# Decoder layer in float32: the last products' sums kept apart, accumulators loaded later

## The chip, the cores and the metric

One core of a Trainium2 chip runs the whole program. The metric is the device time of one execution in microseconds (us). Engines are named PE or TensorE (matmuls), DVE or VectorE, ACT or ScalarE, POOL or GpSimd, and SP, which issues most DMAs.

## The reference

One decoder layer on x of 1024 tokens by 1024 channels, in float32:

```
x <- LN1(alpha*x + 0.5*SwiGLU_1(x))
x <- LN2(alpha*x + W_out [ SparseAttn(x) || ChunkedGMLP(x) ])
x <- LN3(alpha*x + 0.5*SwiGLU_2(x))
SwiGLU(x) = (silu(x @ w1) * (x @ w3)) @ w2        # w1, w3: 1024 x 2816, w2: 2816 x 1024
```

Both SwiGLU layers run through the same function of the kernel; the change is in that function alone. The mixer in the middle (top-k attention and gMLP) is not touched.

## The kernel before

**Precision.** A float32 operand is split into two parts of type fp32r: hi (a ScalarE copy, L87) and lo (the difference, L88, on VectorE or GpSimd). `mm3` (L112 to L114) multiplies with three matmuls: hi by hi, hi by lo, lo by hi.

**Seven products.** `ffn` computes each large product by a 2x2 scheme with seven products of blocks in place of eight (Strassen's, in the form of Winograd). Products are numbered 1 to 7, and the factors and results are sums and differences of blocks.

**First products** (x @ w1, x @ w3). The 2816 hidden channels are 11 groups of two 128-wide blocks. `product(g, m)` is one of the seven products of group g: 24 matmuls into a pair of PSUM banks (tile `ab`; there are two pairs). Products 1 and 2 of groups 0 to 5 run ahead of everything else ("early"); their sums go to DRAM (`spill`), and so does the first part of the hidden block (`hid`). `group(g)` then runs the other products, for g from 1 on in the order 6, 7, 5, 4, 3, adds them on VectorE (u2 at L340, u3 at L375, c at L378), and stores the hidden block to `hid`. Within `group(g)` the next group is loaded: u2 and h1 of an early group (L347, L348) from `spill` and `hid`, and four weight blocks `w` (L300), numbered 1, 2, 7, 4. `left` makes the left factors some three products ahead; S (L248) is the first sum of a group's blocks and needs blocks 7 and 4. Outputs are L402 to L407.

**Second product** (hidden @ w2). Tokens are two halves of four 128-token tiles, the output has two column halves of 512, and k runs over the 11 groups. For each product m but the last, k is the outer loop and the four token tiles j the inner one: 12 matmuls per k. Results gather in four PSUM banks X (tile `y`) for products 1, 2, 5, 4 or four banks Y (tile `z`) for 6, 3, 7. Product 2 may go on top of 1, 7 on top of 3, and 4 on top of 5. For product 4, j is the outer loop (33 matmuls per tile). `prepare` makes the pieces (hi and lo of the hidden block `a` and of the weight block `b`) five ahead; `weights` makes sums of the weight blocks b11, b12, b21, b22 in place on VectorE (L487 to L495). Product 6 needs a sum in a page of its own, `t` (L488).

**Accumulators.** The result is 8 token tiles `xacc` of 1024 columns: C11 and C12 are the column halves of the first four, C21 and C22 of the others. `load_acc` loads alpha*x into them (L591, scaled by ScalarE at L592) in product 1. GpSimd then takes differences (L468, via `each`): C21 - C22 and C22 - C12. `add2` (L530, VectorE) adds half of a product's banks to one quarter: product 1, 6, 5 and 3 to C12, 2 to C11, 7 to C22, 4 to C21. After product 3 GpSimd adds C12 to C22, and after product 7 C22 to C21, which undoes the differences. So what three of the quarters share is added once. `norm` (layernorm) of tiles 0 to 3 runs in product 7, of tiles 4 to 7 after each tile of product 4.

**Order.** Instructions are written in program order and each engine's queue is then ordered by a planner, which simulates the engines with its own costs and takes the earliest in program order among what is ready. Pages (4 KB per partition, 21 of them: weight blocks, factors, pieces, `t`, `xacc`, u2, h1, layernorm rows) and PSUM banks are handed out in that order too. Every engine and the DMA queue of SP run their instructions in order.

Of the kernel before, what the change touches and what calls it, by code (L numbers as in the profile page):

```python
# [12 lines left out]
AF = mybir.ActivationFunctionType  # L13
# [21 lines left out]
class Net:  # L35
# [181 lines left out]
    def ffn(self, name, w13, w2, begin, meanwhile, load_acc, norm, after):  # L217
# [111 lines left out]
        def group(g, begun=None):  # L329
            then = due.append if g == 0 else lambda f: f()  # L330
            if begun:
                h1, h11 = begun
            else:
                a = pair()
                sums[g], h1 = first(g, a), page("h1")
                h11 = h1[:, 0]
            b = pair()
            product(g, 6, b)
            u2 = sums[g]
            then(lambda b=b: V.tensor_tensor(u2, b, sums[g], ALU.add))  # L340
            if not begun:
                product(g, 2, a, start=False)
                gated(h11, a)
            if g < NG - 1:
                if g + 1 < EARLY:
                    sums[g + 1], again[g + 1] = page("u2"), page("h1")
                    nc.sync.dma_start(sums[g + 1], spill[g + 1])  # L347
                    nc.sync.dma_start(again[g + 1][:, 0], hid[g + 1, :, 0])  # L348
                for m in (1, 2, 7, 4):
                    load(g + 1, m)  # L350
            u3, c, h2 = page("u3"), page("c22"), page("h2")
            if g == 0:
                a = pair()
                product(g, 5, a)
                then(lambda: V.tensor_tensor(c, a, u2, ALU.add))
                b = pair()
                product(g, 7, b)

                def out7(b=b):
                    V.tensor_tensor(c, b, c, ALU.add)  # L360
                    V.tensor_tensor(u3, b, u2, ALU.add)
                    gated(h2[:, 1], c)

                then(out7)
                product(g, 3, a, start=False)

                def out3():
                    V.tensor_tensor(u2, a, u2, ALU.add)
                    gated(h2[:, 0], u2)

                then(out3)
            else:
                b = pair()
                product(g, 7, b)
                V.tensor_tensor(u3, b, u2, ALU.add)  # L375
                a = pair()
                product(g, 5, a)
                V.tensor_tensor(c, a, u3, ALU.add)  # L378
                gated(h2[:, 1], c)
            b = pair()  # L380
            product(g, 4, b)
            h12, s4 = (u3[:, 0], u3[:, 1]) if g == 0 else (h1[:, 1], u3[:, 0])

            def out4():
                V.tensor_tensor(u3, b, u3, ALU.add)
                gated(h12, u3)

            then(out4)
            if g:
                product(g, 3, a, start=False)  # L390
                V.tensor_tensor(u2, a, u2, ALU.add)
                gated(h2[:, 0], u2)

            def out():
                e = E(PAR["HE"])
                s = c
                e.tensor_tensor(s[:, 0], h2[:, 0], h2[:, 1], ALU.add)
                e.tensor_tensor(s[:, 1], s[:, 0], h11, ALU.subtract)
                e.tensor_tensor(h2[:, 0], h11, h2[:, 0], ALU.subtract)
                e.tensor_tensor(s4, s[:, 1], h12, ALU.subtract)  # L400
                if g < EARLY:
                    nc.sync.dma_start(hid[g, :, 1], h12)  # L402
                else:
                    nc.sync.dma_start(hid[g, :, 0:2], h1)
                for i, t in enumerate((h2, s), 1):
                    nc.sync.dma_start(hid[g, :, 2 * i : 2 * i + 2], t)
                nc.sync.dma_start(hid[g, :, 6], s4)  # L407

            then(out)
# [53 lines left out]
        for k in range(NG):  # L463
            load2(k)

        def each(e, a, b, op):
            for x, y in zip(a, b):
                e.tensor_tensor(x, x, y, op)  # L468

        order2 = (1, 6, 2, 5, 3, 7, 4)  # L470
        plan2 = [(m, k) for m in order2[:5] for k in range(NG)]
        for k in range(NG + PAR["D4"]):
            if k < NG:
# [1 line left out]
            if k >= PAR["D4"]:  # L475
                plan2.append((4, k - PAR["D4"]))
        HID = {1: 0, 2: 1, 7: 2, 4: 3, 5: 4, 6: 5, 3: 6}
        raws, pieces, last = {}, {}, {}

        def weights(m, k):  # L480

            w = W[k]
            b11, b12, b21, b22 = w[:, 0, 0], w[:, 0, 1], w[:, 1, 0], w[:, 1, 1]
            e = E(PAR["W2S"])
            if m == 6:
                src = self.page("t2", (P, HALF))
                e.tensor_tensor(b11, b12, b11, ALU.subtract)  # L487
                e.tensor_tensor(src, b22, b11, ALU.subtract)  # L488
                return src
            if m == 2:  # L490
                e.tensor_tensor(b12, b22, b12, ALU.subtract)
            if m == 5:
                e.tensor_tensor(b21, b21, b11, ALU.add)
            if m == 3:
                e.tensor_tensor(b21, b22, b21, ALU.subtract)  # L495
            return {1: b11, 2: b21, 5: b11, 3: b22, 7: b12, 40: b21}[m]

        def prepare(n):
# [33 lines left out]
        for m in order2[:6]:  # L532
            if m in (1, 5):
                X = [self.bank("y") for _ in range(4)]
            if m in (6, 3):
                Y = [b[:, s] for b in (self.banks("z") for _ in range(2)) for s in (slice(0, HALF), slice(HALF, D))]
            ps = X if m in (1, 2, 5) else Y
            for k in range(NG):
                prepare(plan2.index((m, k)) + 1 + PAR["LP"])
                for j in range(4):  # L540
                    tile2(m, k, j, ps)
                if m == 1 and k == PAR["AQ"]:
                    acc = load_acc()
                    C11, C12 = ([acc[j][:, s] for j in range(4)] for s in (slice(0, HALF), slice(HALF, D)))
                    C21, C22 = ([acc[4 + j][:, s] for j in range(4)] for s in (slice(0, HALF), slice(HALF, D)))
                    each(E(PAR["CV"]), C21, C22, ALU.subtract)
                    each(E(PAR["CV"]), C22, C12, ALU.subtract)
                if m == 7 and k in PAR["NK"]:
                    t = PAR["NK"].index(k)
                    norm(t, acc[t])  # L550
            for j in range(4):
                add2({2: C11, 7: C22}.get(m, C12)[j], ps[j], -0.5 if m == 3 else 0.5)
            if m == 3:
                each(E(PAR["CV"]), C22, C12, ALU.add)
        each(E(PAR["CV"]), C21, C22, ALU.add)
        for j in range(4):
            for k in range(NG):
                prepare(plan2.index((4, k)) + 1 + PAR["LP"])
                tile2(4, k, j, X)
                if k == PAR["AK"]:  # L560
                    after(j, acc[j])
            add2(C21[j], X[j], -0.5)
            norm(4 + j, acc[4 + j])
        return [lambda t=t: after(t, acc[t]) for t in range(4, NT)]

# [18 lines left out]
                self.nc.tensor.transpose(ps[:, j * P : (j + 1) * P], src[:, k * P : (k + 1) * P], self.ident)  # L584
            self.nc.scalar.activation(self.x_block(((0, 1), (5, 2))[h][b])[:, :, cols], ps.rearrange("p (k c) -> p k c", k=4), AF.Copy)

    def load_acc(self, src):
        acc = []
        for t in range(NT):
            a = self.page("xacc")  # L590
            self.nc.sync.dma_start(a, src[t * P : (t + 1) * P, :])  # L591
            self.nc.scalar.activation(a, a, AF.Copy, scale=ALPHA)  # L592
            acc.append(a)
        return acc
# [542 lines left out]
    def run(self):  # L1137
        nc, ins = self.nc, self.ins
        x1 = self.dram.tile([T, D], F32, tag="x1", name="x1_spill")
        x2 = self.dram.tile([T, D], F32, tag="x2", name="x2_spill")  # L1140
        gb = {}

        def normed(n, dst):
            def norm(t, x):
                if n not in gb:
                    gb[n] = self.rows(f"ln{n}_g"), self.rows(f"ln{n}_b")
                last = n == 3 and t == NT - 1
                cut = PAR["CUT"][3] if last else PAR["CUT"][n - 1]
                self.layernorm(x, x, *gb[n], cut)
                for s in (slice(0, cut), slice(cut, D)) if last else (slice(0, D),):  # L1150
                    nc.sync.dma_start(dst[t * P : (t + 1) * P, s], x[:, s])

            return norm

        nothing = lambda n: None
        tail = self.ffn("f1", ins["ffn1_w13"], ins["ffn1_w2"], self.load_x, nothing, lambda: self.load_acc(ins["x"]), normed(1, x1), self.to_act)
        tail = self.mixer(x1, tail, normed(2, x2), self.to_x)

        def rest(n):
            tail[n]()  # L1160

        self.ffn("f2", ins["ffn2_w13"], ins["ffn2_w2"], nothing, rest, lambda: self.load_acc(x2), normed(3, self.out[0]), lambda t, x: None)


def layouts(i):
# [47 lines left out]
```

## Time and profile before

| | us |
|---|---|
| runs | 1799.16, 1801.49, 1802.94 (median 1801.49) |
| profiled execution | 1801.68 |
| its span | 1799.9 |
| TensorE busy | 1740.1 (97%) |
| VectorE busy | 1326.1 (74%) |
| ScalarE busy | 791.1 (44%) |
| GpSimd busy | 506.6 (28%) |

The span is the time from the first to the last instruction. Matmuls are pipelined, so a busy TensorE is told better by the matmuls in a stretch than by its busy time. The first layer's first products lie at 0 to 436 us, its second at 436 to 658; the last layer's at 1150 to 1573 and 1573 to 1790. The granted clock of TensorE in a stretch is 1.00 at full speed.

### The profile page before, as it was taken

To read this page: it belongs to the slowest core of one execution; us is meant where nothing else is said; L and a number is where in the kernel's file an instruction comes from. 1 tells how busy PE (TensorE), PEld (TensorE's weight loads), DVE (VectorE), ACT (ScalarE), POOL (GpSimd) and SP (SyncE) were. 2 spreads that over 40 slices of the span, in tenths; PEclk is the share of its full clock that TensorE was granted. 3 is DMA by queue.
4 is the path that set the end of the run, shared out by engine and by line. 5 is a ranking of instruction groups with operands and counts; after the bars stand their busy time and mean duration, and the time that the engine had idled before them with its cause. 6 is when DMAs were issued, how large, how long until landed. Compare 5 with 4: busy or idle time off the path is not lost.

```text
span 1799.9 us, 22286 instructions
## 1 busy us (share of the span) xinstructions
PE 1740.1 (97%) x8056; PEld 1459.8 (81%) x8056; DVE 1326.1 (74%) x2192; ACT 791.1 (44%) x1336; POOL 506.6 (28%) x368
## 2 busy tenths in 40 slices
PE   8999999999899999979998999999999999989997
PEld 6878888888788889978876888888788888878886
DVE  5776755666796865999979877877767555589786
ACT  5421322323454435678787763352222222355451
POOL 0013422221400462364247620100323222240035
PEclk9999999999999999989999999999999999999999
DMA  7445432238544332112620006435443322753532
GB/s 282 164 146 193 152 112 88 90 118 324 181 135 134 121 108 56 48 47 65 196 62 13 13 1 204 158 117 203 141 177 127 125 88 88 296 202 113 161 100 82
DMA packets 81790, 235.37 MB, mean 131 GB/s; under 512 B 8208, under 2 KB 8720, under 8 KB 81680
## 3 DMA queue, kind: packets, MB, share of 16 engines
q1 hardware_dynamic: 78320, 225.82, 35.9%
q0 software_dynamic: 1920, 2.89, 0.8%
q10 hardware_dynamic: 1440, 5.24, 0.8%
q8 instruction: 63, 1.03, 0.2%
q14 instruction: 47, 0.39, 0.1%
HBM read 168.64 MB, written 62.39 MB: 128 GB/s over the span
## 4 chain that ended last, share of the span: by engine, by line
PE 80%; DVE 9%; ACT 3%; DMA 3%; issue 3%; POOL 1%; SPq 0%; POOLq 0%; ACTq 0%; DVEq 0%
PE ab L112 14%; PE ab L114 14%; PE ab L113 14%; PE y L113 6%; PE y L112 6%; PE y L114 6%; PE z L113 3%; PE z L114 3%; PE z L112 3%; DMA w<-in_ffn_w_dram 2%; PE tr L986 1%; DVE dve L790 1%; ACT act L799 1%; PE ol L113 1%; PE ol L114 1%
## 5 line engine op out<-in xcount | busy, mean ns | idle before, releaser
L112 PE MATMUL ab<-xs,hi 128*128 128x512 f32 x1232 | 482.6, 392 | 13.4 <-DVE c L378 5.7
L113 PE MATMUL ab<-xs,hi 128*128 128x512 f32 x1232 | 481.8, 391 | 0.0
L114 PE MATMUL ab<-xs,lo 128*128 128x512 f32 x1232 | 481.5, 391 | 0.0
L88 POOL TENSOR_TENSOR lo<-w,hi 128x1024 fp32r<-128x1024 f32 x54 | 135.5, 2509 | 567.7 <-ACT hi L87 527.9
L112 PEld LDWEIGHTS ab<-xs,hi 128*128 128x128 f32 x1232 | 232.8, 189 | 63.3 <-issue 6.4
L113 PEld LDWEIGHTS ab<-xs,hi 128*128 128x128 f32 x1232 | 232.8, 189 | 48.9 <-DVE xs L88 0.4
L114 PEld LDWEIGHTS ab<-xs,lo 128*128 128x128 f32 x1232 | 232.7, 189 | 48.1
L87 ACT ACTIVATE hi<-w 128x1024 fp32r<-128x1024 f32 (+1 forms) x134 | 137.4, 1040 | 184.7 <-DVE w L251 137.1
L88 DVE TENSOR_TENSOR lo<-w,hi 128x1024 fp32r<-128x1024 f32 (+1 forms) x80 | 94.8, 1195 | 41.2 <-ACT hi L87 40.7
L307 ACT ACTIVATE h<-c 128x512 f32<-128x512 f32 x34 | 21.5, 631 | 202.3 <-DVE c L378 141.2
L113 PE MATMUL z<-b,a 128*128 128x512 f32 x264 | 105.2, 398 | 4.0 <-DVE b L88 4.0
L87 ACT ACTIVATE b<-w 128x512 fp32r<-128x512 f32 x110 | 68.9, 626 | 88.2 <-PE y L114 46.4
L112 PE MATMUL z<-b,a 128*128 128x512 f32 x264 | 102.5, 397 | 5.1 <-ACT b L87 5.1
L88 DVE TENSOR_TENSOR a<-hid,a 128x512 fp32r<-128x512 f32 x132 | 95.9, 726 | 12.9 <-ACT a L87 12.9
L114 PE MATMUL z<-b,a 128*128 128x512 f32 x264 | 104.4, 397 | 0.0
L114 PE MATMUL y<-b,a 128*128 128x512 f32 x264 | 102.8, 389 | 0.0
L113 PE MATMUL y<-b,a 128*128 128x512 f32 x264 | 102.8, 389 | 0.0
L799 ACT ACTIVATE act<-score,tk 128x768 int8<-128x768 f32 (+2 forms) x93 | 86.7, 932 | 33.7 <-DVE tk L811 28.8
L112 PE MATMUL y<-b,a 128*128 128x512 f32 x264 | 101.2, 390 | 0.0
L87 ACT ACTIVATE a<-hid 128x512 fp32r<-128x512 f32 x132 | 81.9, 620 | 40.3 <-DMA hid<-f 37.9
L88 DVE TENSOR_TENSOR b<-w,b 128x512 fp32r<-128x512 f32 x110 | 80.2, 730 | 24.1 <-ACT b L87 23.9
L468 POOL TENSOR_TENSOR xacc<-xacc,xacc 128x512 f32<-128x512 f32 x16 | 21.9, 1388 | 237.1 <-DVE xacc L530 236.8
(273 smaller groups left out, 3715.7 us busy)
## 6 DMA issues: line engine op xcount, KB each, us to landing
w<-in_ffn_w_dram SPq DMA_DIRECT2D x110, 512.0 KB, 6.1
hid<-f SPq DMA_DIRECT2D x60, 512.0 KB, 3.8
w<-in_ffn_w_dram SPq DMA_DIRECT2D x22, 1024.0 KB, 11.3
f<-h SPq DMA_DIRECT2D x32, 512.0 KB, 3.4
f<-c SPq DMA_DIRECT2D x22, 512.0 KB, 4.2
xr<-x_spill SPq DMA_DIRECT2D x16, 512.0 KB, 5.3
x_spill<-xr SPq DMA_DIRECT2D x16, 512.0 KB, 3.4
f<-u SPq DMA_DIRECT2D x24, 256.0 KB, 6.0
```

The source lines that it names most:

```text
L87: nc.scalar.activation(hi, src, AF.Copy)
L88: (eng or nc.vector).tensor_tensor(lo, src, hi.bitcast(F32), ALU.subtract)
L112: mm(out, a[0], b[0], start=start, stop=False, skip_group_check=skip)
L113: mm(out, a[0], b[1], start=False, stop=False, skip_group_check=skip)
L114: mm(out, a[1], b[0], start=False, stop=stop, skip_group_check=skip)
L307: nc.scalar.activation(t, c[:, 0], AF.Silu)
L468: e.tensor_tensor(x, x, y, op)
L790: V.tensor_scalar(self.marks("dve", s.shape[-1]), s, f, None, ALU.is_lt, ALU.add, accum_out=val[:, j : j + 1])
L799: nc.scalar.activation(out, s, AF.Sign, bias=fj, scale=-1.0, accum_out=val[:, j : j + 1])
L986: nc.tensor.transpose(pt[:, hh * P : (hh + 1) * P], ps4[hh][:, j * P : (j + 1) * P], self.ident)
```

## The change

1. Product 1's banks are copied by ScalarE, halved, to four half tiles T (two pages). Products 6, 5 and 3 are added to T. After product 3 GpSimd adds T to C12; after product 7 (also added to T) it adds T to C21 and C22. The differences of accumulators and their undoing are gone.
2. The order is 1, 2, 6, 5, 3, 7, 4. The weight sums of the blocks are made in products 2 and 6.
3. `load_acc` takes a range of tiles: four are loaded in product 2 and four in product 5, each at k = 2.
4. In the first products, u2 and h1 of the next early group are requested after this group's last product, no longer ahead of its weight blocks.

```diff
             if g < NG - 1:
-                if g + 1 < EARLY:
-                    sums[g + 1], again[g + 1] = page("u2"), page("h1")
-                    nc.sync.dma_start(sums[g + 1], spill[g + 1])
-                    nc.sync.dma_start(again[g + 1][:, 0], hid[g + 1, :, 0])
                 for m in (1, 2, 7, 4):
                     load(g + 1, m)
...
+            if g + 1 < EARLY:
+                sums[g + 1], again[g + 1] = page("u2"), page("h1")
+                nc.sync.dma_start(sums[g + 1], spill[g + 1])
+                nc.sync.dma_start(again[g + 1][:, 0], hid[g + 1, :, 0])
 
             def out():
...
-        def each(e, a, b, op):
-            for x, y in zip(a, b):
-                e.tensor_tensor(x, x, y, op)
-
-        order2 = (1, 6, 2, 5, 3, 7, 4)
+        order2 = (1, 2, 6, 5, 3, 7, 4)
...
+            if m == 2:
+                e.tensor_tensor(b11, b12, b11, ALU.subtract)
+                e.tensor_tensor(b12, b22, b12, ALU.subtract)
             if m == 6:
                 src = self.page("t2", (P, HALF))
-                e.tensor_tensor(b11, b12, b11, ALU.subtract)
                 e.tensor_tensor(src, b22, b11, ALU.subtract)
+                e.tensor_tensor(b21, src, b21, ALU.subtract)
                 return src
-            if m == 2:
-                e.tensor_tensor(b12, b22, b12, ALU.subtract)
-            if m == 5:
-                e.tensor_tensor(b21, b21, b11, ALU.add)
-            if m == 3:
-                e.tensor_tensor(b21, b22, b21, ALU.subtract)
...
-                if m == 1 and k == PAR["AQ"]:
-                    acc = load_acc()
-                    C11, C12 = ([acc[j][:, s] for j in range(4)] for s in (slice(0, HALF), slice(HALF, D)))
-                    C21, C22 = ([acc[4 + j][:, s] for j in range(4)] for s in (slice(0, HALF), slice(HALF, D)))
-                    each(E(PAR["CV"]), C21, C22, ALU.subtract)
-                    each(E(PAR["CV"]), C22, C12, ALU.subtract)
+                if (m, k) in ((2, 2), (5, 2)):
+                    acc += load_acc(range(len(acc), len(acc) + 4))
...
+            if m == 1:
+                T = [t[:, i] for t in (page("T"), page("T")) for i in range(2)]
             for j in range(4):
-                add2({2: C11, 7: C22}.get(m, C12)[j], ps[j], -0.5 if m == 3 else 0.5)
-            if m == 3:
-                each(E(PAR["CV"]), C22, C12, ALU.add)
-        each(E(PAR["CV"]), C21, C22, ALU.add)
+                if m == 1:
+                    nc.scalar.activation(T[j], ps[j], AF.Copy, scale=0.5)
+                elif m == 2:
+                    add2(acc[j][:, :HALF], ps[j])
+                else:
+                    add2(T[j], ps[j], -0.5 if m == 3 else 0.5)
+                if m == 3:
+                    nc.gpsimd.tensor_tensor(acc[j][:, HALF:], acc[j][:, HALF:], T[j], ALU.add)
+                if m == 7:
+                    for s in (slice(0, HALF), slice(HALF, D)):
+                        nc.gpsimd.tensor_tensor(acc[4 + j][:, s], acc[4 + j][:, s], T[j], ALU.add)
...
-            add2(C21[j], X[j], -0.5)
+            add2(acc[4 + j][:, :HALF], X[j], -0.5)
```

## Rows read from the trace of the kernel before

**Rows 1.** Slices: length, busy us (count) of PE, PEld, DVE, ACT, POOL; clock; DMA.
```profile
125.00:150.00 25.00, 21.41 (x84) 17.23 (x83) 15.72 (x16) 6.74 (x8) 10.02 (x4) 0.86 0.52 178
...
450.00:475.00 25.00, 22.45 (x99) 18.00 (x97) 18.82 (x29) 11.66 (x16) 19.12 (x8) 1.00 0.63 232
475.00:500.00 25.00, 23.00 (x91) 18.78 (x91) 21.96 (x37) 14.10 (x25) 0.00 (x0) 0.86 0.41 116
500.00:525.00 25.00, 25.00 (x112) 20.72 (x111) 25.00 (x43) 12.51 (x22) 0.00 (x0) 1.00 0.33 95
525.00:550.00 25.00, 25.00 (x112) 20.73 (x111) 21.17 (x35) 11.84 (x21) 0.00 (x0) 1.00 0.58 171
...
575.00:600.00 25.00, 25.00 (x112) 20.73 (x111) 20.63 (x31) 13.68 (x24) 5.49 (x4) 1.00 0.40 127
...
1250.00:1275.00 25.00, 22.93 (x102) 18.69 (x101) 18.78 (x18) 6.13 (x7) 4.81 (x2) 1.00 0.53 189
1600.00:1625.00 25.00, 20.44 (x79) 16.15 (x78) 18.04 (x28) 8.94 (x16) 11.65 (x8) 0.86 0.31 90
```

**Rows 2.** Waits of TensorE: line, what for, us in total, times, longest.
```profile
PE ab L112 <- DVE c L378: 5.7, 2, 3.6
...
PE z L112 <- ACT b L87: 5.1, 2, 2.6
PE z L113 <- DVE b L88: 4.0, 2, 2.0
```

**Rows 3.** TensorE in order of time, product 6: start, us, instruction.
```profile
477.66 0.63 PE L114 MATMUL z<-b,a 128*128 128x512 f32 x1
478.09 0.63 PE L112 MATMUL z<-b,a 128*128 128x512 f32 x1
```

**Rows 4.** VectorE in order of time, in brackets the idle time before.
```profile
466.79 0.69 DVE L530 SCALAR_TENSOR_TENSOR xacc<-y,xacc 128x512 f32<-128x512 f32 x1 [2.56 <-POOL xacc L468]
...
472.41 1.13 DVE L488 TENSOR_TENSOR t<-w 128x512 f32<-128x512 f32 x1
...
536.08 0.69 DVE L530 SCALAR_TENSOR_TENSOR xacc<-y,xacc 128x512 f32<-128x512 f32 x1
```

**Rows 5.** GpSimd in order of time: first and last of eight differences.
```profile
455.39 10.01 POOL L468 TENSOR_TENSOR xacc<-xacc 128x512 f32<-128x512 f32 x1 [36.67 <-ACT xacc L592]
...
473.07 1.60 POOL L468 TENSOR_TENSOR xacc<-xacc,xacc 128x512 f32<-128x512 f32 x1
```

**Rows 6.** Groups by line: count, then shortest, median and longest ns of one.
```profile
L468 POOL TENSOR_TENSOR xacc<-xacc x16: 1275/1296/10007, 455.4 to 1769.9; 128x512 f32<-128x512 f32 x16
...
L933 ACT ACTIVATE yf<-y x6: 575/577/601, 869.2 to 906.6; 128x512 f32<-128x512 f32 x6
...
L488 DVE TENSOR_TENSOR t<-w x22: 674/684/1131, 459.3 to 1626.4; 128x512 f32<-128x512 f32 x22
```

**Rows 7.** SP's queue in order of time, group 1 of the first products.
```profile
101.80 0.34 SPq L347 DMA_DIRECT2D u<-f_c  x1
107.81 0.33 SPq L402 DMA_DIRECT2D f<-u  x1
...
109.97 0.37 SPq L300 DMA_DIRECT2D w<-in_ffn_w_dram  x1
...
111.87 1.15 SPq L300 DMA_DIRECT2D w<-in_ffn_w_dram  x2
```

**Rows 8.** One stretch, columns as in rows 1; last the DMA share and GB/s.
```profile
107.80:121.50 13.70, 13.70 (x62) 11.37 (x61) 7.56 (x9) 1.06 (x1) 0.00 (x0) 1.00 0.91 324
```

**Rows 9.** VectorE in order of time, group 1 of the first products.
```profile
121.49 1.23 DVE L248 TENSOR_TENSOR S<-w,w 128x1024 f32<-128x1024 f32 x1 [5.77 <-DMA w<-in_ffn_w_dram]
...
127.56 1.22 DVE L378 TENSOR_TENSOR c<-ab,u 128x1024 f32<-128x1024 f32 x1
```

**Rows 10.** All engines in order of time, product 3: splits of one piece.
```profile
1717.06 0.63 ACT L87 ACTIVATE b<-w 128x512 fp32r<-128x512 f32 x1 [1.57 <-PE z L114]
...
1718.33 0.69 DVE L88 TENSOR_TENSOR a<-hid,a 128x512 fp32r<-128x512 f32 x1
```

More of the change, by code (lines that the diff above doesn't have):

```diff
@@ L477, in ffn @@
         HID = {1: 0, 2: 1, 7: 2, 4: 3, 5: 4, 6: 5, 3: 6}
-        raws, pieces, last = {}, {}, {}
+        raws, pieces, last, acc = {}, {}, {}, []
         def weights(m, k):
@@ L585, in to_x, with load_acc @@
             self.nc.scalar.activation(self.x_block(((0, 1), (5, 2))[h][b])[:, :, cols], ps.rearrange("p (k c) -> p k c", k=4), AF.Copy)
-    def load_acc(self, src):
+    def load_acc(self, src, tiles):
         acc = []
-        for t in range(NT):
+        for t in tiles:
             a = self.page("xacc")
@@ L1155, in run @@
         nothing = lambda n: None
-        tail = self.ffn("f1", ins["ffn1_w13"], ins["ffn1_w2"], self.load_x, nothing, lambda: self.load_acc(ins["x"]), normed(1, x1), self.to_act)
+        tail = self.ffn("f1", ins["ffn1_w13"], ins["ffn1_w2"], self.load_x, nothing, lambda ts: self.load_acc(ins["x"], ts), normed(1, x1), self.to_act)
         tail = self.mixer(x1, tail, normed(2, x2), self.to_x)
@@ L1160, in rest @@
             tail[n]()
-        self.ffn("f2", ins["ffn2_w13"], ins["ffn2_w2"], nothing, rest, lambda: self.load_acc(x2), normed(3, self.out[0]), lambda t, x: None)
+        self.ffn("f2", ins["ffn2_w13"], ins["ffn2_w2"], nothing, rest, lambda ts: self.load_acc(x2, ts), normed(3, self.out[0]), lambda t, x: None)
 def layouts(i):
```

## The prediction

> **What bounds the kernel now.** I read the time of each engine in slices of 25 us first. Outside the mixer, the start and the tail, a slice holds 112 matmuls in 25.00 us, so one matmul costs 25.00/112 = 0.2232 us, and TensorE is the bound. Four places hold fewer [rows 1]: 125:150 has 84; 450:475 and 475:500 have 99 and 91; 1250:1275 has 102; 1600:1625 has 79. They miss 28, 34, 10 and 33 matmuls, or 6.2, 7.6, 2.2 and 7.4 us: 23.4 us in all. No other slice of the two feed-forward layers, past their first 50 us and before the tail, is short.
>
> Then the waits of TensorE name the places [rows 2]: `ab <- DVE c L378`, twice, is in the first products; `z <- ACT b L87` and `z <- DVE b L88`, twice each, are in the second.
>
> Place A, second products, once per layer. TensorE starts product 6, waits 2.6 us for the upper half of a right factor, then 2.0 us for its lower half [rows 2], and the matmuls behind stand 0.43 us apart [rows 3], not 0.22: that is the 1.2 GHz level, and slice 475:500 shows a granted clock of 0.86 [rows 1]. Backwards: the factor `t` (L488) starts on VectorE at 472.41, behind the sums of product 1 (L530), which waited for GpSimd, 2.56 us the first time and once more after it [rows 4]. GpSimd's eight differences of accumulators began at 455.39 with one of 10.01 us and ended at 474.67 [rows 5]; the median of one is 1.296 us [rows 6]. The second layer repeats it.
>
> Place B, first products, group 1. SP issues u2 of group 2 at 101.80, then stands behind an output (L402) until 107.81; h1 and the four weight blocks follow, the second block at 109.97, the last two from 111.87 [rows 7]. The DMA engines are 0.91 busy from 107.80 to 121.50, moving 324 GB/s [rows 8]. S (L248) waits 5.77 us on VectorE for these blocks, starts at 121.49, and c (L378), the read that product 3 needs, stands behind it until 127.56 [rows 9]. The second layer loses 2.2 us so, without a slow stretch.
>
> **The change part by part.** Durations and the sum are those of the profiled execution: its time is 1801.68 us, 0.19 above the median of the three runs.
>
> *Differences of accumulators go; product 1 goes to T through ScalarE.* The wait of L530 on GpSimd goes with L468, and nothing behind it on VectorE is held: place A, -7.6 and -7.4. Added are four copies from PSUM per layer; the nearest row, a ScalarE copy of the same shape, is 0.577 us [rows 6]. Product 2 now accumulates on product 1's banks, so its first matmul into a bank waits for that bank's copy. Above: all four in the open, 2.3 us per layer. Below: nothing, since the kernel before already drains these banks just ahead of reuse (product 2, then 5: four sums, the last at 536.08 [rows 4]) and slice 525:550 holds 112 matmuls [rows 1]. A gain is excluded, as TensorE has no idle time there. I take 0. What hides it: a bank's last matmuls come 3, 6 and 9 matmuls before the product's end. If ScalarE stands on a late hid transfer just then, that cover is gone, and up to 2.3 us show.
>
> *Order 1, 2, 6 and the weight sums.* Per k, before: one in 2, two in 6, one in 5, one in 3. After: two in 2, two in 6. VectorE loses 11 x 0.684 = 7.5 us of work per layer (duration of L488 [rows 6]), in stages where it isn't the limit: 0. The dense stage is now product 6, with two splits and two sums per k, 4 x 0.60 = 2.4 us (starts in a row are 0.60 apart), against 12 x 0.2232 = 2.68 us of matmuls. The kernel before had four per k in product 2: slice 500:525 shows VectorE 25.00 of 25.00 with 112 matmuls [rows 1]. Above: the sum for b21 in the open once per k, 11 x 0.6 = 6.6 us per layer; nearest is that full slice, so 0.
>
> *Accumulators later.* Eight transfers and eight scalings by ScalarE per layer move from product 1 to products 2 and 5, past the hid loads on SP's queue. ScalarE is at 12.51 and 11.84 of 25 there [rows 1], with room for four scalings at a time. 0; above, one late hid pair, some 3 us.
>
> *Pages.* There are 21. Before: 8 accumulators, 12 for six pieces, one `t`. From product 5 on: 2 of T and 8 accumulators leave 11, so five pieces, not six. A piece is 2.68 us of matmuls, and from a freed page to a ready piece it takes from 1717.06 to 1719.02, some 2.0 us [rows 10]. Two pieces suffice; five are there: 0. The upper end is the slower rival.
>
> *GpSimd's adds of T.* Four after product 3, as before, but now the layernorms of tiles 0 to 3 need them; eight after product 7, not four, in front of tiles 4 to 7. The first four were done in 5.49 us, in slice 575:600 [rows 1]. The eight cost 8 x 1.296 = 10.4 us; tile 4 needs two of them (2.6 us) within 33 matmuls (7.4 us), and product 4 gives each tile its own bank, so TensorE doesn't wait. The tail after the last matmul has none of them. 0; above, the second rival.
>
> The Trainium skill, "SBUF — State Buffer", Who interferes with whom, says that a VectorE instruction with two SBUF inputs keeps a GpSimd instruction that reads SBUF off the shared port pair for its whole length. By it each add would wait as long as VectorE's stream has no gap. The 10.01 us row agrees, the four in 5.49 us don't, so by the rule the time is the second rival's; by the rows it is the forecast's.
>
> *u2 and h1 issued after the weight blocks.* The blocks take u2's place at 101.80 and h1's; the last, which S needs, goes out where the second did, at 109.97 instead of after 111.87: 1.9 us earlier. It also runs ahead of 768 KB, which at 324 GB/s is 2.4 us. S so comes between 2.4 us (a full pipe alone) and 4.3 us (both) earlier. The waits to cover are 3.6 and 2.1 us (5.7 in all, the longest 3.6 [rows 2]). The second layer's goes whole, -2.2. The first's leaves 0 to 1.2 us, and without a long wait the slow stretch goes too (the second layer's 2.1 us had none: its 10 missing matmuls are 2.2 us): I take 0.7 left, -5.5. Lower end: S is put earlier on VectorE too, and nothing is gained. Late next are u2 and h1, issued some 4 us later; they are read only after product 6 of the next group, 20 us on. The same edit in groups 0 and 2 to 4, where TensorE doesn't wait, gives 0. Nothing is queued behind them on SP but this group's outputs.
>
> Sum: 1801.68 - 7.6 - 7.4 - 5.5 - 2.2 = 1779.0 us.
>
> **Rivals.**
> *Only place A goes.* The instruction order is made by a planner which knows no queueing of four transfers; it may move S forward by as much as the loads gain. For: S waits 5.77 us now, so the planner already has it too early. Against: S's place after L375 follows the program's order, which stays. Time: 1801.68 - 15.0 = 1786.7.
>
> *The wait on GpSimd comes back.* Product 3's adds are starved as the first difference was; tile 0's statistics wait on VectorE, and splits behind them. Price as in place A, 7.6 and 7.4: 1779.0 + 15.0 = 1794.0. For: the 10.01 us row. Against: VectorE was at 20.63 of 25 there, not full, and five pieces are ready.
>
> *Slower: the pages run dry.* In products 5 and 3, with T and all accumulators held, each piece may wait for the page of the one before, and 2.0 us of splitting stand in the open. There are 44 such pieces in two layers; the change is slower once over 12 of them stand (23.4/2.0). Half of them: 1778.3 + 22 x 2.0 = 1822. For: 8 + 12 + 1 already fill all 21 pages. Against: five ready pieces are 13 us of matmuls, and VectorE has less to do there than before.
>
> *It doesn't do what it says*: TensorE finds another wait in each place, and the time stays at about 1800.
>
> **How the numbers follow.** Forecast 0.57, only place A 0.18, GpSimd's wait back 0.14, no change 0.04, slower 0.07. A measurement here tells about 0.2%, 3.6 us, from no change. Faster: 0.57 + 0.18 + 0.14 = 0.89; same 0.04; slower 0.07. The range takes in the first three cases: the low end, 1775, is the sum with place B wholly gone (1778.3) and 3 us of shifts in the mixer, whose order is planned anew; the high end, 1794, is GpSimd's wait back.
>
> **What would show it.** Right: slices of the second products from product 1's end to product 4 with 112 matmuls each, no wait of TensorE on `t`, four ScalarE copies of about 0.58 us at the end of product 1, no GpSimd work in product 1; in group 1 of the first products, the block loads ahead of u2, S starting at 117 to 119 and TensorE waiting under 1.2 us for c. Wrong: a wait of TensorE on an X bank (the copies), on `a` or `b` in products 5 and 3 (pages), of VectorE's statistics on an add of T (GpSimd), or S still at 121. A wait of either kind above 2 us per layer makes the forecast wrong; so would a shift of the mixer by more than 4 us.

## The result and the profile after

The kernel after takes 1787.94 us, the median of four runs (1787.11 to 1792.4), beside 1801.99 (1799.16 to 1802.94) for the kernel before on the same chip: 0.993 of it, with an interval of 0.9909 to 0.995. It is faster, as forecast, inside the range of 1775 to 1794, and 8.9 us above the forecast of 1779.0.

The profiled execution took 1787.14 us, with a span of 1785.4 (before: 1799.94). Cut at the first and last matmul of each stage, the two spans compare so (us; "forecast" is the prediction's term):

| stage | before | after | difference | forecast |
|---|---|---|---|---|
| first products, layer 1 | 436.26 | 432.36 | -3.90 | -5.5 |
| second products, layer 1 | 220.61 | 212.93 | -7.68 | -7.6 |
| mixer | 492.37 | 495.53 | +3.16 | 0 |
| first products, layer 2 | 424.16 | 423.57 | -0.59 | -2.2 |
| second products, layer 2 | 217.06 | 209.60 | -7.46 | -7.4 |
| after the last matmul | 9.48 | 11.41 | +1.93 | 0 |
| sum | 1799.94 | 1785.40 | -14.54 | -22.7 |

Slices of the kernel after, in the columns of [rows 1]:

```profile
125.00:150.00 25.00, 22.40 (x99) 18.56 (x100) 21.67 (x18) 6.53 (x9) 10.13 (x4) 1.00 0.50 179
...
425.00:450.00 25.00, 25.00 (x112) 20.71 (x111) 25.00 (x40) 11.59 (x22) 0.00 (x0) 1.00 0.54 189
450.00:475.00 25.00, 25.00 (x112) 20.67 (x112) 19.74 (x34) 17.67 (x30) 0.00 (x0) 1.00 0.71 236
475.00:500.00 25.00, 25.00 (x112) 20.71 (x111) 22.95 (x39) 11.45 (x20) 0.00 (x0) 1.00 0.34 105
500.00:525.00 25.00, 25.00 (x112) 20.71 (x111) 23.37 (x39) 14.68 (x26) 0.00 (x0) 1.00 0.56 177
525.00:550.00 25.00, 25.00 (x112) 20.68 (x111) 11.03 (x18) 12.58 (x19) 0.00 (x0) 1.00 0.65 214
575.00:600.00 25.00, 25.00 (x112) 20.71 (x111) 24.28 (x44) 13.34 (x24) 11.54 (x8) 1.00 0.31 103
1250.00:1275.00 25.00, 23.52 (x104) 19.15 (x104) 20.44 (x16) 6.76 (x8) 10.15 (x4) 1.00 0.52 192
1600.00:1625.00 25.00, 25.00 (x112) 20.71 (x111) 19.86 (x33) 15.12 (x26) 0.00 (x0) 1.00 0.42 130
```

Every slice of the second products now holds 112 matmuls, where [rows 1] had 99, 91 and 79, and no wait of TensorE is left in them. The first products still have their short slices, though the first one's clock is 1.00 here and was 0.86. TensorE's waits in the first products of layer 1, then of layer 2 (before: 3.6 and 2.1, [rows 2]):

```profile
PE ab L112 <- DVE c L374: 2.6, 1, 2.6
...
PE ab L112 <- DVE c L374: 1.5, 1, 1.5
```

SP's queue, its wait by name, and VectorE in group 1 of the first products, the rows that answer to [rows 7] and [rows 9]:

```profile
107.44 0.32 SPq L403 DMA_DIRECT2D f<-u  x1
107.86 1.36 SPq L300 DMA_DIRECT2D w<-in_ffn_w_dram  x3
...
110.76 0.33 SPq L300 DMA_DIRECT2D w<-in_ffn_w_dram  x1
...
SPq L403 <- DVE u L308: 17.7, 1, 17.7
...
120.16 1.23 DVE L248 TENSOR_TENSOR S<-w,w 128x1024 f32<-128x1024 f32 x1 [4.80 <-DMA w<-in_ffn_w_dram]
...
126.24 1.22 DVE L374 TENSOR_TENSOR c<-ab,u 128x1024 f32<-128x1024 f32 x1
```

u2 and h1 no longer stand ahead of the blocks, yet no block leaves before 107.86: SP stands 17.7 us behind group 0's output (L403), which waits for VectorE. S gains 1.33 us (121.49 to 120.16), not the 2.4 to 4.3 forecast.

The tail, GpSimd and then VectorE in order of time:

```profile
1751.07 10.48 POOL L554 TENSOR_TENSOR xacc<-xacc,T 128x512 f32<-128x512 f32 x8
1761.51 0.54 POOL L134 TENSOR_TENSOR rstd<-rs,mhalf 128x1 f32<-128x1 f32 x1
...
1762.09 0.16 DVE L135 TENSOR_TENSOR rs<-rstd 128x1 f32<-128x1 f32 x1 [4.18 <-POOL rstd L134]
...
1774.95 0.68 DVE L524 SCALAR_TENSOR_TENSOR xacc<-y,xacc 128x512 f32<-128x512 f32 x1
```

GpSimd does all eight adds in one row, 10.48 us. The `rstd` of tile 4's layernorm, a GpSimd step (L134), stands behind the last of them, VectorE idles 4.18 us for it, and the layernorms of tiles 5 to 7 follow late. The last sum starts at 1774.95, though the last matmul ended at 1773.99.

### The profile page after: what moved, and what is told of

The parts are those of the page before. It is cut to its first block, busy times and chain, and to the rows that moved or that the text cites. A ratio compares the mean times of both kernels' runs of the same rounds, so it can differ in the third digit from the quotient of the medians.

```text
span 1785.4 us, 22226 instructions
## 1 busy us (share of the span) xinstructions
PE 1733.3 (97%) x8056; PEld 1455.8 (82%) x8056; DVE 1326.0 (74%) x2162; ACT 792.8 (44%) x1344; POOL 482.1 (27%) x360
## 4 chain that ended last, share of the span: by engine, by line
PE 75%; DVE 13%; DMA 3%; issue 3%; POOL 3%; ACT 3%; SPq 0%; POOLq 0%; DVEq 0%; ACTq 0%
PE ab L112 14%; PE ab L113 14%; PE ab L114 14%; PE y L112 4%; PE y L114 4%; PE y L113 4%; DVE dve L789 2%; PE z L112 2%; PE z L114 2%; PE z L113 2%; DMA w<-in_ffn_w_dram 2%; PE tr L985 1%; POOL xacc L554 1%; ACT act L798 1%; PE ol L113 1%
## 5 line engine op out<-in xcount | busy, mean ns | idle before, releaser
L88 POOL TENSOR_TENSOR lo<-w,hi 128x1024 fp32r<-128x1024 f32 x54 | 136.9, 2535 | 562.0 <-ACT hi L87 504.9
L88 DVE TENSOR_TENSOR lo<-w,hi 128x1024 fp32r<-128x1024 f32 (+1 forms) x80 | 94.7, 1194 | 41.0 <-ACT hi L87 40.2
L88 DVE TENSOR_TENSOR a<-hid,a 128x512 fp32r<-128x512 f32 x132 | 93.6, 709 | 25.3 <-ACT a L87 25.3
L551 POOL TENSOR_TENSOR xacc<-xacc,T 128x512 f32<-128x512 f32 x8 | 13.0, 1651 | 333.8 <-DVE T L524 333.8
L113 PE MATMUL z<-b,a 128*128 128x512 f32 x264 | 102.7, 389 | 0.0
L114 PE MATMUL z<-b,a 128*128 128x512 f32 x264 | 102.7, 389 | 0.0
L112 PE MATMUL z<-b,a 128*128 128x512 f32 x264 | 102.5, 389 | 0.0
L88 DVE TENSOR_TENSOR b<-w,b 128x512 fp32r<-128x512 f32 x110 | 77.3, 703 | 33.8 <-ACT b L87 33.6
```

What stands on the lines that cost most here:

```text
L88: (eng or nc.vector).tensor_tensor(lo, src, hi.bitcast(F32), ALU.subtract)
L112: mm(out, a[0], b[0], start=start, stop=False, skip_group_check=skip)
L113: mm(out, a[0], b[1], start=False, stop=False, skip_group_check=skip)
L114: mm(out, a[1], b[0], start=False, stop=stop, skip_group_check=skip)
L551: nc.gpsimd.tensor_tensor(acc[j][:, HALF:], acc[j][:, HALF:], T[j], ALU.add)
```

## The experiments

Twelve kernels; each time is a median beside the kernel before on the same chip, whose medians were 1800.57 to 1802.44. Stage lengths come from each one's profile, cut as in the table.

### Place A: what made it?

**Order alone**, in the kernel before:

```
-        order2 = (1, 6, 2, 5, 3, 7, 4)
+        order2 = (1, 2, 6, 5, 3, 7, 4)
   (weight sums of m = 2 and 6 as in the kernel after; accumulators and differences as before)
```

> The kernel before with the order 1, 2, 6, 5, 3, 7, 4 and the sums of weights that go with it; accumulators and their differences on GpSimd as before. It tells what the order alone is worth. Theory: none; product 2 now accumulates on the banks that product 1's sums (VectorE, behind GpSimd's differences) drain, so TensorE waits for them directly instead of for t: those sums ended near 472 us and product 1 near 470 us, so a wait of 2 to 5 us per layer stays with the slow clock behind it, and the time is 1796 to 1806, no better than 1800.8. Rival: the order itself (t two products later) makes most of place A's gain: 1785 to 1789.

Measured: 1797.11, ratio 0.9981 (0.9965 to 0.9997); second products 216.35 and 212.78. TensorE's waits in layer 1:

```profile
PE y L112 <- DVE xacc L527: 2.5, 2, 2.0
```

The wait turned from `t` to the banks themselves, as expected, and is about half as long (2.5 us in layer 1, 4.6 before). The slow clock that was expected behind it doesn't follow, so the order alone is worth something after all: 4.3 us per layer.

**Differences on VectorE**, in the kernel before:

```
-'CV': 1
+'CV': 0
```

> The kernel before, with the differences of accumulators (L468) computed by VectorE instead of GpSimd; nothing else. Theory: place A is made by GpSimd's slowness at them (1.296 us each, the first 10.01 us), for which VectorE's sums of product 1 wait 2.56 us and more; VectorE does a difference in 0.684 us, so the eight cost it 5.5 us, of which it gets back its own waits. PE's wait for t in product 6 then falls from 4.6 us to under 2 us per layer and the slow clock behind it goes: about 1788 to 1793, against 1800.8 of the kernel before. Rival: any difference of accumulators ahead of the sums of product 1 is too much there, since VectorE is the limit of that stretch: t comes as late as before, and the time stays within 3 us of 1800.8. In both the 8 accumulators are loaded early.

Measured: 1797.14, ratio 0.9968 (0.9953 to 0.9983); second products 216.98 and 212.24. TensorE's wait in layer 1, and the slices:

```profile
PE z L113 <- DVE b L88: 1.8, 1, 1.8
...
450.00:475.00 25.00, 23.15 (x98) 18.44 (x97) 25.00 (x43) 13.32 (x18) 0.00 (x0) 0.97 0.67 250
475.00:500.00 25.00, 25.00 (x108) 20.63 (x107) 23.15 (x40) 15.95 (x28) 0.00 (x0) 0.96 0.48 136
```

The wait fell from 4.6 to 1.8 us, as the theory had it. The time sits between theory and rival: VectorE is now full (25.00 of 25), and a shorter wait and some slow clock remain. Taking the differences off GpSimd gains 3.6 and 4.8 us, half to two thirds of place A.

**Accumulators early**, in the kernel after:

```
-                if (m, k) in ((2, 2), (5, 2)):
-                    acc += load_acc(range(len(acc), len(acc) + 4))
+                if m == 1 and k == PAR["AQ"]:
+                    acc += load_acc(range(NT))
```

> The kernel after, with all eight accumulators loaded and scaled in product 1 (at k = 4), as before the change, instead of four in product 2 and four in product 5. Theory: the later loads are worth nothing, since nothing but pages hangs on them: second products 212.9 and 209.6 us, time within 2 us of the kernel after (1787.9). Rival: the pages run dry when eight accumulators and two pages of T are held from product 1 on (11 left for pieces): up to 13 of the pieces in products 2, 6, 5 stand for 2.0 us each in each layer, 1800 and more.

Measured: 1794.09, ratio 0.9961 (0.9945 to 0.9977); second products 215.99 and 212.22. Both theory (no cost) and rival (pages) fell. TensorE's wait in layer 1; the slices of product 1; the times from issue to landing of the hid transfers from 440 to 466 us; then, on ScalarE, the last conversion that waits for hid and the copies to T:

```profile
PE y L112 <- ACT T L545: 2.7, 1, 2.7
...
425.00:450.00 25.00, 25.00 (x112) 20.71 (x111) 24.24 (x40) 14.55 (x25) 0.00 (x0) 1.00 0.77 285
450.00:475.00 25.00, 22.29 (x99) 18.10 (x98) 16.52 (x27) 16.22 (x25) 0.00 (x0) 1.00 0.71 253
...
DMA to landing us min/median/max: 3.6/6.6/9.1
...
463.70 0.63 ACT L87 ACTIVATE a<-hid 128x512 fp32r<-128x512 f32 x1 [1.90 <-DMA hid<-f]
...
466.84 2.03 ACT L545 ACTIVATE T<-y 128x512 f32<-128x512 f32 x4
```

The same times to landing in the kernel after:

```profile
DMA to landing us min/median/max: 2.7/4.0/7.0
```

TensorE waits for the copies to T, which start at 466.84, 32.2 us after the product's first matmul; in the kernel after it is 28.8. They stand on ScalarE behind conversions of hid that came late: among the transfers of the accumulators, those of hid take 6.6 us at the median, 4.0 without them. ScalarE's wait for hid in total doesn't tell this. From 432 to 466 us it is 9.1 us here and 16.8 in the kernel after, where ScalarE has less to do in between.

**The same, scaled by GpSimd** instead of ScalarE:

```
-            self.nc.scalar.activation(a, a, AF.Copy, scale=ALPHA)
+            self.nc.gpsimd.tensor_scalar(a, a, ALPHA, None, ALU.mult)
```

> The kernel after with all eight accumulators loaded in product 1, as in the kernel measured at 1794.1, but scaled by GpSimd instead of ScalarE. It tells which of the two early costs makes TensorE wait 2.7 and 2.3 us for the copies to T. Theory: the hid transfers, late because the accumulators' 4 MB share the DMA engines with them, make the factors late that stand ahead of the copies on ScalarE; the wait stays, 1792 to 1795. Rival: the eight scalings by ScalarE (1.06 us each, 8.5 us) push the copies back; they go, the wait with them, 1787 to 1789.

Measured: 1796.03, ratio 0.9963 (0.9948 to 0.9978); second products 215.33 and 211.45; TensorE's wait in layer 1, and the same two rows of ScalarE:

```profile
PE y L112 <- ACT T L545: 2.1, 1, 2.1
...
461.13 0.63 ACT L87 ACTIVATE a<-hid 128x512 fp32r<-128x512 f32 x1 [2.84 <-DMA hid<-f]
...
464.27 2.03 ACT L545 ACTIVATE T<-y 128x512 f32<-128x512 f32 x4
```

The theory's wait stayed (the time is 1 us above its range). TensorE waits 2.1 and 1.5 us in the two layers, where it was 2.7 and 2.3. In both kernels the copies start 3.14 us after the conversion that waited for hid, in either layer, so ScalarE's scalings don't push them back. The 0.6 and 0.8 us less are hid transfers that landed that much earlier; why they did isn't shown. What makes the wait is hid, which shares the DMA engines with 4 MB of accumulators. The copies to T without the new order were not run, so the shares of these two in place A are not told apart.

### Place B: what are the loads worth?

**Second products only** (u2 and h1 issued ahead of the blocks again, in the kernel after):

```
             if g < NG - 1:
+                if g + 1 < EARLY:
+                    sums[g + 1], again[g + 1] = page("u2"), page("h1")
+                    nc.sync.dma_start(sums[g + 1], spill[g + 1])
+                    nc.sync.dma_start(again[g + 1][:, 0], hid[g + 1, :, 0])
                 for m in (1, 2, 7, 4):
...
-            if g + 1 < EARLY:
-                ...
```

> The change to the second products alone; u2 and h1 of the next early group are issued ahead of its weight blocks, as in the kernel before. Theory: each second product loses its wait of TensorE on the factor t (7.6 and 7.4 us, 220.6 -> 212.9 us and 217.1 -> 209.6 us from its first matmul to its last), the end after the last matmul grows by 1.9 us (eight adds of T on GpSimd), and the first products keep their loss (84 and 102 matmuls in the two short slices): 1801.7 - 15.1 + 1.9 = 1788.5 us. Rival: the 3.2 us that the mixer took longer in the changed kernel belong to this edit (pages, later accumulators): then 1791.7, with a mixer of 495.5 us instead of 492.4 in the profile.

Measured: 1790.34, ratio 0.9944 (0.9931 to 0.9957), between theory and rival. **Loads only** is the reverse, the move alone in the kernel before:

> The later issue of u2 and h1 alone, with the second products of the kernel before. Theory: first products 436.3 -> 432.4 us and 424.2 -> 423.6 us, S on VectorE some 1.3 us earlier, nothing else: 1801.7 - 4.5 = 1797.2 us, and place A keeps its 7.6 and 7.4 us. Rival: the mixer's 3.2 us come with this edit: 1800.4 us.

Measured: 1798.67, ratio 0.999 (0.998 to 1.0), again between the two. Both put the move at about 2 us (1800.77 - 1798.67; 1790.34 - 1787.94), but the interval of the second reaches 1.0, and those of the first and of the kernel after overlap: it isn't clear of noise. The mixer took 494.90 and 494.88 us in these two profiles, so neither edit is needed for its longer time. TensorE's waits in group 1 are 3.3 and 1.9 us with the loads as before, 2.5 and 1.8 with them moved. Whether the slow clock follows changes by execution: the same load code gave 99 matmuls at 1.00 in the slice 125:150 of the kernel after and 85 at 0.86 with half of the adds on VectorE (below). That stretch is most of the -3.90 in the table: 15 matmuls, 3.3 us, of which the wait is 1.0.

**Outputs on ScalarE's queue** (group 0's, in the kernel after):

```
+                q = nc.scalar if g == 0 else nc.sync
                 if g < EARLY:
-                    nc.sync.dma_start(hid[g, :, 1], h12)
+                    q.dma_start(hid[g, :, 1], h12)
                 ...
-                    nc.sync.dma_start(hid[g, :, 2 * i : 2 * i + 2], t)
-                nc.sync.dma_start(hid[g, :, 6], s4)
+                    q.dma_start(hid[g, :, 2 * i : 2 * i + 2], t)
+                q.dma_start(hid[g, :, 6], s4)
```

> The changed kernel with the outputs of group 0 (four DMAs) issued by ScalarE and not by SP. Theory: in group 1 the weight blocks of group 2 stand behind such an output on SP (17.7 us, until h12 is made) and share the DMA engines with the others, so S comes at 120.2 us; free of it, three blocks are issued from about 102 us on, and with 0.5 MB less in the crowd (1.6 us at 323 GB/s) S comes at 118.6 us or before: TensorE's waits for c fall from 2.6 and 1.5 us to under 1 and 0, time 1784.5 us. Rival: the blocks wait for pages, not for SP: their issue stays at 107.9 us, the waits too, time 1787.9 us.

Measured: 1781.13, ratio 0.9898 (0.9882 to 0.9913); first products 429.55 and 421.81. SP, VectorE, and the two slices that were short:

```profile
101.53 4.00 SPq L300 DMA_DIRECT2D w<-in_ffn_w_dram  x4
...
115.37 1.22 DVE L248 TENSOR_TENSOR S<-w,w 128x1024 f32<-128x1024 f32 x1
...
125.00:150.00 25.00, 25.00 (x112) 20.71 (x111) 19.16 (x17) 5.29 (x6) 9.01 (x4) 1.00 0.56 201
1250.00:1275.00 25.00, 25.00 (x112) 20.72 (x111) 16.89 (x16) 6.87 (x8) 9.65 (x4) 1.00 0.48 179
```

The four blocks leave from 101.53, S waits for nothing, and both slices are full. SP's order was the cause. Of the profile's 7.5 us against the kernel after (span 1777.9 against 1785.4), 2.8 and 1.8 lie in the first products; 2.95 lie in the mixer, where this profile has the shorter of two lengths (see The mixer), so the edit itself is worth some 4.6. **The same with the loads as before** tells what the move adds then:

> The kernel after with group 0's outputs issued by ScalarE, and with u2 and h1 of the next group issued ahead of the weight blocks, as before the change. It tells whether the move of u2 and h1 is worth anything once SP no longer stands behind an output. Theory: what delayed the blocks was SP's wait alone; with u2 and h1 ahead again the blocks start some 2.4 us (768 KB at 324 GB/s) later than with the outputs on ScalarE and the move, S at about 117.8 instead of 115.4, before VectorE and TensorE need it: no wait for c above 0.5 us, time 1781 to 1782. Rival: the 768 KB ahead are a term of their own, a wait of 1 to 2.5 us for c comes back in each layer, with a slow clock behind the first: 1784 to 1788.

Measured: 1783.71, ratio 0.9892 (0.9865 to 0.9918); first products 429.33 and 421.81, S at 115.49 after a wait of 0.25, and no wait of TensorE for c. S is there earlier than the theory's 117.8, and the move is worth nothing in the first products. The time lies between theory and rival. Its profile is 4.6 us longer than that with the move (span 1782.5 against 1777.9), and 4.5 of them lie in the mixer (497.07 against 492.58).

### The tail

**Half of the last adds on VectorE**, in the kernel after:

```
-                        nc.gpsimd.tensor_tensor(acc[4 + j][:, s], ...
+                        (nc.gpsimd if s.start else V).tensor_tensor(acc[4 + j][:, s], ...
```

> The changed kernel with the four adds of T to the C21 halves on VectorE; GpSimd keeps the four of the C22 halves, as many as it had after product 7 before the change. Theory: the eight adds in a row (10.5 us) held the power instruction of tile 4's layernorm and pushed those of tiles 5 to 7; with four the end after the last matmul falls from 11.4 to 9.5 us: 1787.9 - 1.9 = 1786.0 us. Rival: the end grew because VectorE was late for tile 7 by its own work: then the four adds more on VectorE leave it at 11.4 us or make it longer, 1788 us or more.

Measured: 1787.57, ratio 0.993 (0.9917 to 0.9943); after the last matmul 9.5 us. GpSimd now has four in a row, and `rstd` of tile 4 waits for VectorE's step before it, not for them:

```profile
1753.72 6.47 POOL L554 TENSOR_TENSOR xacc<-xacc,T 128x512 f32<-128x512 f32 x4
1761.34 0.99 POOL L134 TENSOR_TENSOR rstd<-rs,mhalf 128x1 f32<-128x1 f32 x1 [1.15 <-DVE rs L133]
```

The 1.93 us are gone, so the adds made them; the median doesn't show it. The profiled execution (1787.53, near the median) had the slow stretch in the first products: 436.19 us, 432.36 in the kernel after. **Both edits**, these adds and the outputs:

> The kernel after with group 0's outputs issued by ScalarE and with the adds of T to the left halves of the last four accumulators on VectorE. If the two gains add: 1781.1 (outputs alone) less the tail's 1.9 = 1779.2, with S of group 1 not waiting, a tail of 9.5 us after the last matmul and all slices of the products full. Rival: the four adds cost VectorE in product 7 or 4 what they give back at the end: 1781.

Measured: 1779.32, ratio 0.9876 (0.9854 to 0.9898), span 1776.2, of it 9.5 after the last matmul, no wait of TensorE for c or in the second products. The gains add. It beats both kernels.

### The mixer

The change doesn't touch it, and its instructions stand in the same order on each engine. GpSimd's split of two wo blocks (L88) and VectorE's scan (L851 before, L850 after), first before, then after:

```profile
994.43 6.73 POOL L88 TENSOR_TENSOR wo<-wo,wo 128x1024 fp32r<-128x1024 f32 x2
996.66 2.32 DVE L851 TENSOR_TENSOR_SCAN rank<-eq 128x1024 f32<-128x1024 bf16 x1
```

```profile
982.71 4.76 POOL L88 TENSOR_TENSOR wo<-wo,wo 128x1024 fp32r<-128x1024 f32 x2
985.22 4.40 DVE L850 TENSOR_TENSOR_SCAN rank<-eq 128x1024 f32<-128x1024 bf16 x1
```

Before, the pair of splits took 6.73 us and the scan 2.32; after, 4.76 and 4.40. One of the two loses some 2 us, and which one is a matter of tenths of a us. In the twelve profiles so far (before, after and ten experiments) the scan took 4.2 to 4.5 us in five (mixer 494.9 to 497.1) and 2.3 in seven (492.4 to 493.6). TensorE's first matmul behind the scan and the 3.5 us from it on (columns as in [rows 1]), before and after:

```profile
999.90 0.41 PE L112 MATMUL sc<-cTh,act 128*128 128x320 f32 x1 [1.04 <-DVE m L973]
...
999.90:1003.40 3.50, 3.50 (x22) 3.14 (x23) 3.50 (x9) 2.19 (x4) 3.03 (x3) 1.00 0.00 0
```

```profile
990.53 0.63 PE L112 MATMUL sc<-cTh,act 128*128 128x320 f32 x1 [3.19 <-DVE m L972]
...
990.50:994.00 3.50, 3.47 (x14) 3.07 (x14) 3.50 (x9) 1.03 (x2) 1.82 (x2) 0.54 0.00 0
```

The scan holds up `m` on VectorE, TensorE waits 2.15 us longer for it, and behind that wait the granted clock is 0.54. Counted from the mixer's first matmul, TensorE's work in the kernel after is 0.2 us late ahead of this place and 3.2 us late behind it: this is the +3.16 of the table. In all five profiles with a long scan this wait is 2.9 to 3.4 us and the clock behind it slow; in the seven with a short one the wait is 1.0 us. **A later split**, to steer it, in the kernel after:

```
+        if late:
+            eng.memset(lo[:, :HALF].bitcast(F32), 0.0)
         self.split(raw, hi, lo, eng)
   (late for the fourth wo block only)
```

> The kernel after, with one more instruction on GpSimd: it writes zeros to half of the lower part of the fourth wo block just ahead of the split that overwrites it, so that this split starts some tenths of a us later. Theory: the mixer's 3.2 us come from a race; where GpSimd's split starts first (by 0.13 us in the kernel after), VectorE's scan of 1024 elements takes 4.4 us instead of 2.32. With the split later the scan starts first, takes 2.3 us, the split waits instead, and the mixer takes 492.4 to 493.6 us, as in the seven profiles with a short scan: span about 1783 for 1785.4, and the time 1784 to 1788. Rival: the scan's length is a sign and not the cause, or what the split then loses is as late: the mixer stays at 494.9 to 497 us, and the time at 1788 or above.

Measured: 1790.46, ratio 0.9936 (0.9915 to 0.9957); mixer 496.42:

```profile
992.75 2.38 POOL L88 TENSOR_TENSOR wo<-wo,wo 128x1024 fp32r<-128x1024 f32 x1
993.42 3.85 DVE L852 TENSOR_TENSOR_SCAN rank<-eq 128x1024 f32<-128x1024 bf16 x1
```

The planner moved the work of VectorE and TensorE with the new instruction, and the split again came first, by 0.67 us. The attempt to steer failed, but the row tells the mechanism: the scan ends at 997.27, 2.14 us after the split's end at 995.13; in the kernel after it ends at 989.62, 2.15 after 987.47. A scan that runs first takes 2.3 us, so this one does nearly all its work after the split. **With both edits of the best kernel**:

> The kernel measured at 1779.3 (group 0's outputs on ScalarE, the left adds of T on VectorE), with the same extra instruction on GpSimd. Its profile had the short scan already (2.30 us, mixer 492.9 us). Theory: the profile's span stays within 1.5 us of 1776.2, and the median falls by 0 to 2 us, by as many executions as had the long scan. Rival: the instruction costs something of its own: 1781 or more.

Measured: 1780.51, ratio 0.988 (0.9859 to 0.9902), span 1778.8, the scan 3.70 us, mixer 493.76. It gains nothing, and the span misses the theory's 1776.2 by 2.6 us, of which 1.7 lie in the first products. The scan is long and the mixer still near the short ones'. TensorE's work around the scan has been moved here too: its wait behind the scan is 2.61 us, and the clock of the 3.6 us after it stays at 1.00 (with the later split alone 2.75 us, then 0.76). A long scan thus costs what TensorE waits for it and what the clock does then, not a fixed sum.

## Why the prediction was right or wrong

**Place A, -7.6 and -7.4: right in size (-7.68, -7.46), only half right in cause.** The step put it all down to L468: "The wait of L530 on GpSimd goes with L468, and nothing behind it on VectorE is held". Taking GpSimd out of product 1 gives 3.6 and 4.8 us, the order alone 4.3 and 4.3, and the whole change to these products with the accumulators early 4.6 and 4.8: the two don't add. Only with the accumulators later is the place empty.

**"Accumulators later", 0: wrong, 3.1 and 2.6 us of those gains** (215.99 - 212.93; 212.22 - 209.60). The step looked at ScalarE's room and missed what the accumulators do on the DMA engines. With them early, a hid transfer takes 6.6 us to land at the median and not 4.0: they make hid late, hid the conversions on ScalarE, and these the copies to T. That chain stood in the prediction, as what takes the copies' cover away ("If ScalarE stands on a late hid transfer just then"); the later loads are what keeps it away. The sum came out right because the term of place A had been read from the gap, whatever made it.

**Copies, order and weight sums, pages, 0 each: right as costs.** The copies take 0.592 us (0.577 forecast) and no bank is waited for; full slices throughout. That the order was also worth 4.3 us per layer by itself, out of place A, the prediction didn't see.

**GpSimd's adds, 0: wrong by +1.93.** After product 3 they were starved in part, as the rival said, to 1.74 us at the median for a form that takes 1.29 alone, but nothing waited for them. Those after product 7 held VectorE's statistics 5.8 us in four waits (2.5 in layer 1, 3.3 in layer 2), without a wait of TensorE. By the prediction's own sign, such a wait above 2 us per layer makes the forecast wrong; here no matmul waited for it, and the price came in the tail alone. After product 7 the step "The tail after the last matmul has none of them" failed. It watched the adds, not the layernorm of tile 4, whose GpSimd step is queued behind them on an in-order engine, with three more layernorms behind that.

The Trainium skill ("SBUF — State Buffer", Who interferes with whom) was weighed there. The 1.74 us agree that GpSimd's reads lose time beside VectorE, but 0.45 us each, not a whole stream's length.

**Place B, -5.5 and -2.2: mis-sized, -3.90 and -0.59, of which the waits are 1.0 and 0.6.** The step "It also runs ahead of 768 KB" failed first. u2's 512 KB left at 101.80 and took 3.2 us from issue to landing, and the DMA engines of the kernel before then stood idle:

```profile
104.80:107.80 3.00, 3.00 (x15) 2.50 (x14) 3.00 (x6) 2.53 (x3) 0.00 (x0) 1.00 0.00 0
```

The last two columns of this stretch, share and GB/s, are zero. So only h1's 256 KB, 0.8 us at 324 GB/s, were in the crowd of [rows 8]. Then "The blocks take u2's place at 101.80" failed: they start at 107.86, because they stand behind the output (L402, L403 after) on SP, as in [rows 7]; u2 alone had stood ahead of it. The prediction had that wait in its reading of [rows 7] and left it out of the term, and S came at 120.16, not at 117 to 119. The clock's share comes or goes with the execution: the first short slice was slow in three of four profiles with the loads as before, in two of six with them moved, too few to give it to the move.

**The mixer, 0 within 3 us: +3.16.** The range had allowed 3 us of shifts there, downward; it came upward, from a scan that lost a race to GpSimd in this profile: a wait of TensorE 2.15 us longer, and a slow clock behind it.

**Rivals.** The pages did not run dry. "Only place A goes" gave 1786.7, 1.2 us from the median. That is luck: its mechanism, the planner putting S earlier, wasn't the one that kept S late (SP's queue was), and place B did give 4.5 us, which the mixer's 3.2 and the tail's 1.9 took back.

**The time within the range.** Place A came as forecast. Place B, the mixer and the tail together came 8.3 us above their terms, and the time still lies in the range because its high end was set for GpSimd's wait coming back, which it didn't. So the range held for another reason than the one given.

## What to carry to other kernels

A gap's size can be forecast from the gap; which of the changes closes it can't, so take them one at a time. When transfers are moved forward on an in-order queue, look first for the instruction on it that waits: here moving group 0's outputs to another queue took TensorE's waits for c out of the first products (2.8 and 1.8 us from the kernel after), and moving loads ahead of loads was then worth nothing. When side work goes to an idle engine, list what else that engine has to do in the same stretch, small steps of a chain above all.

## What the runs showed of the hardware

- VectorE's scan of 128x1024 elements took 2.3 us where it started first and 3.7 to 4.5 where a GpSimd split of 2.4 us had started first, by up to 0.84 us: in all seven profiles with a long scan it ends 2.14 to 2.15 us after the split. Where the scan is first, the split loses the time instead (6.73 us for a pair, not 4.76). The Trainium skill ("SBUF — State Buffer", Who interferes with whom) says of VectorE with two inputs and GpSimd's reads that the one to start second stands for the other's whole length; these rows agree (the scan's two inputs are both eq).
- Waits of 2.5 to 3.7 us of TensorE in group 1 of the first products were followed by a slow clock in five profiles and not in five others: 0.86 granted in the slice after 2.9, 3.1, 3.5, 3.6 and 3.7 us, 1.00 after 2.5, 2.6, 2.7, 3.2 and 3.3. The length of the wait alone doesn't decide it.
- GpSimd's scaling of a 128x1024 accumulator took 3.3 us at the median and 4.6 on average (2.8 to 16.7), ScalarE's 1.06.
